# Loads of the inverses' layout issued from GpSimd's queue, with two planner estimates changed, in a hybrid decoder layer

## The chip, the core and the metric

The kernel runs on one core of one Trainium2 chip. That core has five engines which run side by side, each through its own list of instructions and strictly in the order of that list: TensorE (PE in the profile, with PEld for its weight loads), VectorE (DVE), ScalarE (ACT), GpSimd (POOL) and SyncE (SP, which here only starts transfers). Any of SP, ACT and POOL can start a DMA transfer; the instruction that starts it takes its place in that engine's list. The metric is the device time of one execution in microseconds (us).

## The reference

The layer takes x (1024 tokens by 2048), normalises it, multiplies it by one combined projection `W_in`, and feeds the columns to three groups of heads: a spatial gMLP (4 groups of 128 channels), a gated DeltaNet (8 heads of 128) and a cross-attention into 256 memory tokens (4 heads of 128). Each group's output is gated by SiLU of its own columns, all is multiplied by `W_out`, added to x and normalised. The part that the change touches is the DeltaNet. Cut to that:

```python
qkv = causal_conv_silu(concat([d_q, d_k, d_v]), conv_w)      # width-4 convolution over tokens
q, k = l2norm(q) * DN_HEAD_DIM ** -0.5, l2norm(k)
# gated_delta_rule, in chunks of C = 64 tokens
a = where(strict, einsum('bhnid,bhnjd->bhnij', k * beta, k) * decay, 0.0)
T = triangular_solve(a + eye, eye, left_side=True, lower=True, unit_diagonal=True)   # inverse of I + a
value       = einsum('bhnij,bhnjd->bhnid', T, v * beta)
k_cumdecay  = einsum('bhnij,bhnjd->bhnid', T, k * beta * exp(g_cum))
attn_intra  = where(tri, einsum('bhnid,bhnjd->bhnij', q, k) * decay, 0.0)
def step(state, inp):                     # one chunk after the other, along the sequence
    v_new = val_c - k_cumdecay_c @ state
    o_c   = q_g_c @ state + attn_intra_c @ v_new
    state = state * exp(g_last) + k_dec_c.T @ v_new
```

All is in float32, which the kernel makes of products of high and low parts (three matmuls for one, `ahi,whi`, `ahi,wlo`, `alo,whi` in the profile).

## The kernel before, in words

**Who sets the order.** No engine's list is written by hand. The kernel's body calls `S`, `G`, `V`, `PE`, `Q` (ACT, POOL, DVE, PE, SP), and these only record each operation in a `Plan`, with the earlier operations that it depends on. When all is recorded, `Plan.issue` walks through the operations as a planner would: at each step it takes the engine that is free first and, of that engine's operations whose inputs are there by its own clock, the one with the lowest class (`rank(n)` sets the class; 1 is urgent, 9 is the main matmul stream) and then the earliest recorded. It appends this one to the engine's list. What it thinks of times are the estimates in `Plan.price`: `o.cost` is how long an operation occupies its engine, `o.lat` how much later its result is there. For transfers there is also a size term: those of SP and POOL share one modelled channel, those of ACT have a channel of their own at half its rate. On the chip, the lists are then run as they stand: an estimate that is off costs no correctness, but moves operations to other places in the lists, on every engine. All recorded operations are issued through one line, so the profile shows line 280 for nearly everything, and the tiles' names tell them apart.

**Stages.** From 0 to about 165 us the memory tokens are projected and x is normalised. From then to about 500 us the kernel projects the columns of DeltaNet heads 0 to 3, first for tokens 0 to 511 ("half 0", inverses named 00 and 01, two heads each) and then for tokens 512 to 1023 ("half 1", 10 and 11), and runs the DeltaNet on them between the projections' matmuls. From there to about 1310 us five rounds of products (`blocks`) compute the remaining columns by a seven-product scheme; between these matmuls lie the fronts of the late heads 4 to 7 (near 690 and 880 us), one joint inverse for all of these, their recurrences (near 1000 to 1200 us), the gMLP and the attention. From about 1310 us to the end the output projection runs, with no DeltaNet work in it.

**One pair of heads.** `front` does the convolution (`conv`: ACT copies a finished bank of the projection, `xr<-acc`, then three DVE passes), the norms, the decays and, for two heads, the tile `gt` (128 partitions by 8 chunk pairs by 128) that holds the matrices `a`. `blocks_out` then sends the 32x32 blocks on the diagonal of `gt` to DRAM, in four transfers from ACT's queue (`gdr<-gt`), of 32 KB each in pieces of 128 bytes. `inverse` loads them again in another layout, one 32x32 block to a partition, in four transfers (`gd` in the code, a slot of the ring `inv`, so `inv<-gdr` in the profile; 8 partitions by 1024 numbers each), prepares an identity `ti` on POOL, and inverts all blocks at once in 31 steps of two DVE instructions. The results go to DRAM (`tdr`, `udr`, again from ACT's queue). `levels` loads them into place and assembles the 128x128 inverses `ut` by four groups of small matmuls with ACT copies between (`tblk`, `y1`, `y2`). `scan_step`, once for each chunk pair of 128 tokens, is the recurrence: matmul `dn<-states,kT`, then DVE `steps<-dn,sc,vs`, matmul `dn<-steps,ut`, then ACT `steps<-dn`, matmuls `dn<-steps,kd` and `dn<-steps,ai`, and DVE `states<-states,sc,dn`. The joint inverse of the late heads is the same code with four pairs, so 16 loads and 128 partitions.

The loads `gd` run on ACT's queue before, and are recorded with class 1; so are the four stores ahead of them. There are 32 of those stores in the program (8 pairs) and 32 of these loads. The planner's estimates that the change touches stand in `price` at the name "dma_start": the cost of issuing a transfer on each engine, and the latency of a transfer into DRAM.

Of the kernel before, what the change touches and what calls it, by code (L numbers as in the profile page):

```python
# [62 lines left out]
class Plan:  # L63
# [21 lines left out]
    @contextmanager  # L85
    def rank(self, cls):
        old, self.cls = self.cls, cls
        yield
        self.cls = old
# [91 lines left out]
    def price(self, o, name, outs, ins):  # L181

        out = outs[0]
        n = math.prod(out.shape[1:])
        both = [*outs, *ins]
        psum = any(i.space == PSUM for i in both)
        pointer = any(i.shape[-1] == 1 and math.prod(i.shape[1:]) == 1 for i in ins[1:])
        o.nbytes = o.lock = 0
        o.lat = 0.0
        if name == "dma_start":  # L190
            o.cost = {"sp": 380.0, "act": 100.0, "pool": 800.0}[o.eng]
            rows = math.prod(out.shape[:-1])
            o.nbytes = max(4 * math.prod(out.shape), 512 * rows)
            src = ins[0]
            pieces = src.shape[-1] < 128 or out.shape[-1] < 128
            if out.space == DRAM:
                o.lat = 3000.0
            elif pieces or out.shape[0] < 32:
                o.lat = 2400.0
            elif list(src.ap)[0][0] == 0:  # L200
                o.lat = 4000.0
        elif o.eng == "pe":
            passes = 1 if ins[0].dtype == F32R else 2 if name == "transpose" else 4
            o.cost = max(13.3 + n / 2.4 * passes, 222.0 if passes == 4 else 110.0) if out.shape[0] == P else 30.0
            o.lat = 175.0
        elif o.eng == "act":
            o.cost = (165.0 if psum else 200.0) + 0.82 * n + (105.0 if pointer else 0.0)
            o.cost += 190.0 if "accum_out" in o.kw else 0.0
        elif o.eng == "dve":
            n = max([n] + [math.prod(i.shape[1:]) for i in ins])  # L210
            o.cost = (n + 151) / 0.96 + (60.0 if pointer and name == "scalar_tensor_tensor" else 0.0)
            o.lock = not psum and (name.startswith("tensor_") or name == "scalar_tensor_tensor")
            o.lock = o.lock and name != "tensor_reduce"
        else:
            o.lock = 1
            if name in ("memset", "affine_select"):
                o.cost = 100.0 + 0.83 * n * (1 if name == "memset" else 1.4)
                o.lat = 800.0 if name == "affine_select" else 0.0
            else:
                o.cost = 750.0 + 150.0 * (n - 1) if n < 8 else 200.0 + 2.1 * n  # L220
# [63 lines left out]
def kernel(  # L284
# [21 lines left out]
    x, mem, w_in, out = x[0], mem[0], w_in[0], out[0]  # L306
# [7 lines left out]
    V, S, G, PE, Q = R.dve, R.act, R.pool, R.pe, R.sp  # L314
# [5 lines left out]
    def DT(shape, name, dt=F32):  # L320
        return dr.tile(list(shape), dt, name=name, tag=name)[:]
# [35 lines left out]
    def bc(ap, n):  # L357
        return ap.unsqueeze(ap.ndim).to_broadcast(list(ap.shape) + [n])

    def rep(ap, n):  # L360
        return ap.unsqueeze(1).to_broadcast([ap.shape[0], n, ap.shape[1]])
# [618 lines left out]
    def flat(start, *aps):  # L980
        start(*(a.rearrange("p a b -> p (a b)") for a in aps))

    def inverse(gdrs, n, cls):

        nr = 32 * len(gdrs)
        gd = ring["inv"]()[0:nr].rearrange("p (a b) -> p a b", b=32)
        for i, gdr in enumerate(gdrs):
            for b in range(4):
                with rank(1):
                    flat(S.dma_start, gd[i * 32 + b * 8 : i * 32 + (b + 1) * 8], gdr[b])  # L990
        ti = ring["inv"]()[0:nr].rearrange("p (a b) -> p a b", b=32)
        tmp = (y1 if nr == 32 else y2)[0:nr].rearrange("p c m -> p (c m)")
        with rank(4):
            G.memset(ti, 0.0)
            G.affine_select(out=ti, in_=ti, compare_op=ALU.not_equal, fill=1.0, base=0,
                            pattern=[[1, 32], [-1, 32]], channel_multiplier=0)
        with rank(cls):
            for j in range(31):
                n1, m = 31 - j, j + 1
                tv = tmp[:, 0 : n1 * m].rearrange("p (n m) -> p n m", m=m)  # L1000
                V.tensor_tensor(out=tv, in0=bc(gd[:, j, j + 1 :], m), in1=rep(ti[:, j, 0:m], n1), op=ALU.mult)
                V.tensor_tensor(out=ti[:, j + 1 :, 0:m], in0=ti[:, j + 1 :, 0:m], in1=tv, op=ALU.add)
            V.tensor_copy(gd.rearrange("p i m -> p m i"), ti)
        tdr, udr = ([DT([32, 32, 32], f"{t}{n}_{i}") for i in range(len(gdrs))] for t in ("tdr", "udr"))
        for i in range(len(gdrs)):
            with rank(1):
                flat(S.dma_start, tdr[i], ti[i * 32 : (i + 1) * 32])
                flat(S.dma_start, udr[i], gd[i * 32 : (i + 1) * 32])
        return list(zip(tdr, udr))
# [181 lines left out]
    def inverted(n, *states):  # L1191
        return [(*s[:-1], i) for s, i in zip(states, inverse([s[-1] for s in states], n, 3))]
# [324 lines left out]
    with rank(2.6):  # L1517
        late_inv = inverse(gdrs, "late", 1.9)
# [265 lines left out]
```

## Time and profile before

| | |
|---|---|
| median of 3 runs | 1671.42 us (1670.85, 1671.42, 1673.37) |
| span of the profiled execution | 1664.6 us |
| mean granted TensorE clock in it | 0.992 of full speed |
| PE busy | 1623.0 us, 98% of the span |
| DVE busy | 1317.2 us, 79% |
| ACT busy | 1023.2 us, 61% |
| POOL busy | 108.1 us, 6% |
| moved by DMA | 419.50 MB, 252 GB/s |

The profile gives for the profiled execution its span and no other time; the median of the runs is 6.8 us above that span. Times in the timeline count from the span's start. A line of a timeline reads: start, duration, engine (ACTq is an issue of a transfer on ACT), line, operation, output<-inputs, shape, how many alike follow each other, and in brackets the idle time of the engine ahead of it with what ended that. A line of a table by windows reads: window, its length, then busy time and instructions of PE, PEld, DVE, ACT, POOL, then the granted clock of PE, the busy share of the DMA engines and the GB/s. In a table of waits a line gives total us, how many, and the longest.

### The profile page before, as it was taken

Reading aid. Unit: us, or ns where it says so; the run is one execution under the profiler, and the core shown is the slowest. Engines: PE = TensorE matmul, PEld = TensorE weight load, DVE = VectorE, ACT = ScalarE, POOL = GpSimd, SP = SyncE. Lnnn points to the kernel's source line nnn. Section 1 sums busy time; section 2 is a strip of 40 time slices with the busy share of each in tenths; the row PEclk is TensorE's granted clock in tenths of the full one; section 3 lists DMA queues with packets and bytes.
Section 4 is the critical chain, followed back from the end, with each engine's and each line's share of the span. In section 5 each row is a group of like instructions: output and inputs, shape, how many; then the busy total and the mean of one; then the engine's idle time right before and its main releaser. Section 6 shows DMA issues by size and latency. Waiting matters only on the chain.

```text
span 1664.6 us, 26198 instructions
## 1 busy us (share of the span) xinstructions
PE 1623.0 (98%) x8570; PEld 1355.5 (81%) x8570; DVE 1317.2 (79%) x2288; ACT 1023.2 (61%) x2235; POOL 108.1 (6%) x139
## 2 busy tenths in 40 slices
PE   8999999989999999999998999999999999999997
PEld 6888888878878888788886887888888888888886
DVE  4866696939779789889996988786878897688875
ACT  6957674656754457776674447676566774345445
POOL 0000100101010001010010011000000000000001
PEclk9999999999999999999998999999999999999999
DMA  8878887885886877679876877888868869679746
GB/s 273 253 235 267 270 254 225 245 235 180 266 286 208 256 247 250 201 264 326 291 245 206 264 233 242 261 279 282 301 220 291 269 219 359 213 254 304 226 141 240
DMA packets 316658, 419.50 MB, mean 252 GB/s; under 512 B 57773, under 2 KB 138342, under 8 KB 316522
## 3 DMA queue, kind: packets, MB, share of 16 engines
q1 hardware_dynamic: 304834, 410.48, 76.4%
q10 hardware_dynamic: 10600, 5.26, 1.2%
q0 software_dynamic: 1088, 2.10, 0.4%
q8 instruction: 67, 1.10, 0.3%
q14 instruction: 69, 0.57, 0.1%
HBM read 334.33 MB, written 82.87 MB: 251 GB/s over the span
## 4 chain that ended last, share of the span: by engine, by line
PE 72%; DMA 7%; DVE 5%; ACT 2%; issue 2%; ACTq 0%; SPq 0%; POOL 0%; POOLq 0%; DVEq 0%
PE acc L280 54%; PE dn L280 18%; DMA wraw<-in_w_in_dram 1%; DVE alo L280 1%; DMA E<-gcd 1%; DVE y L280 1%; DVE wlo L280 1%; DMA inv<-gdr 1%; DMA y<-in_w_in_dram 1%; ACTq L280 0%; ACT ahi L280 0%; DMA raws<-sd 0%; DVE ai L280 0%; DVE inv L280 0%; DMA zg<-hTd 0%
## 5 line engine op out<-in xcount | busy, mean ns | idle before, releaser
L280 PE MATMUL acc<-ahi,whi 128*128 128x512 f32 (+1 forms) x1152 | 452.9, 394 | 3.3 <-ACT xr L280 1.8
L280 PE MATMUL acc<-alo,whi 128*128 128x512 f32 (+1 forms) x1152 | 452.8, 393 | 0.0
L280 PE MATMUL acc<-ahi,wlo 128*128 128x512 f32 (+1 forms) x1152 | 451.5, 392 | 0.4 <-DVE small L280 0.4
L280 PEld LDWEIGHTS acc<-ahi,whi 128*128 128x128 f32 x1152 | 217.9, 189 | 46.8 <-ACT xr L280 3.1
L280 PEld LDWEIGHTS acc<-ahi,wlo 128*128 128x128 f32 x1152 | 217.7, 189 | 41.2 <-DVE wlo L280 0.6
L280 PEld LDWEIGHTS acc<-alo,whi 128*128 128x128 f32 x1152 | 217.9, 189 | 40.5
L280 PE MATMUL acc<-ahi,zh 128*128 128x512 f32 x736 | 232.1, 393 | 0.0
L280 ACT CAST whi<-wraw 128x512 fp32r<-128x512 f32 (+1 forms) x170 | 137.2, 809 | 112.6 <-PE acc L280 67.7
L280 DVE TENSOR_TENSOR alo<-raws,ahi 128x1024 fp32r<-128x1024 f32 x131 | 160.0, 1222 | 39.3 <-ACT ahi L280 38.9
L280 DVE TENSOR_TENSOR wlo<-wraw,whi 128x1024 fp32r<-128x1024 f32 (+1 forms) x138 | 135.0, 979 | 61.2 <-ACT whi L280 58.4
L280 ACT CAST ahi<-raws 128x1024 fp32r<-128x1024 f32 x131 | 137.4, 1049 | 67.0 <-PE dn L280 28.1
L280 PEld LDWEIGHTS acc<-ahi,zh 128*128 128x128 f32 x736 | 137.0, 188 | 27.1
L280 PE MATMUL acc<-ahi,zl 128*128 128x512 f32 x368 | 144.7, 393 | 0.0
L280 DVE TENSOR_TENSOR ahi<-y,ahi 128x1024 fp32r<-128x1024 f32 x65 | 79.3, 1220 | 23.9 <-ACT ahi L280 23.6
L280 ACT CAST ahi<-y 128x1024 fp32r<-128x1024 f32 x65 | 68.2, 1049 | 37.4 <-PE acc L280 18.3
L280 PEld LDWEIGHTS acc<-ahi,zl 128*128 128x128 f32 x368 | 69.2, 188 | 13.5
L280 ACT CAST zh<-wraw 128x1024 fp32r<-128x1024 f32 x36 | 37.8, 1051 | 44.1 <-PE acc L280 19.9
L280 POOL TENSOR_TENSOR small<-small,mhalf 128x1 f32<-128x1 f32 x26 | 18.6, 721 | 676.9 <-DVE small L280 676.9
L280 POOL TENSOR_TENSOR hs<-hs,mhalf 128x4 f32<-128x4 f32 x32 | 48.4, 1516 | 204.4 <-DVE hs L280 203.4
L280 ACT CAST whi<-y 128x1024 fp32r<-128x1024 f32 x34 | 35.8, 1052 | 38.8 <-issue 20.4
L280 PE MATMUL dn<-wlo,ahi 128*128 128x512 f32 x152 | 59.0, 389 | 0.0
L280 PE MATMUL dn<-whi,alo 128*128 128x512 f32 x152 | 59.0, 389 | 0.0
(397 smaller groups left out, 3221.1 us busy)
## 6 DMA issues: line engine op xcount, KB each, us to landing
wraw<-in_w_in_dram SPq DMA_DIRECT2D x268, 256.0 KB
raws<-sd SPq DMA_DIRECT2D x148, 256.0 KB
y<-in_w_in_dram SPq DMA_DIRECT2D x92, 256.0 KB
y<-sd SPq DMA_DIRECT2D x77, 256.0 KB
wraw<-in_w_out_dram SPq DMA_DIRECT2D x64, 256.0 KB
raws<-h0d SPq DMA_DIRECT2D x54, 256.0 KB
y<-in_w_out_dram SPq DMA_DIRECT2D x33, 256.0 KB
low<-wlo SPq DMA_DIRECT2D x32, 256.0 KB
```

Source lines behind the costliest of these rows:

```text
L280: o.fn(*o.args, **o.kw)
```

## The change

Three edits. `inverse` issues its loads from POOL (`G`) where ACT (`S`) did. In `price`, the estimated cost of issuing a transfer goes from 100 to 430 ns on ACT and from 800 to 1000 ns on POOL. And a transfer into DRAM whose shape is (32, 8, 32), which only the four stores of `blocks_out` have, is estimated to land 9000 ns after its issue and size term, where it was 3000. The arithmetic, the tiles and the sizes of all transfers stay as they are.

```diff
@@ class Plan, def price
         if name == "dma_start":
-            o.cost = {"sp": 380.0, "act": 100.0, "pool": 800.0}[o.eng]
+            o.cost = {"sp": 380.0, "act": 430.0, "pool": 1000.0}[o.eng]
             rows = math.prod(out.shape[:-1])
             o.nbytes = max(4 * math.prod(out.shape), 512 * rows)
             src = ins[0]
             pieces = src.shape[-1] < 128 or out.shape[-1] < 128
             if out.space == DRAM:
-                o.lat = 3000.0
+                o.lat = 9000.0 if out.shape == (32, 8, 32) else 3000.0
@@ def inverse
         for i, gdr in enumerate(gdrs):
             for b in range(4):
                 with rank(1):
-                    flat(S.dma_start, gd[i * 32 + b * 8 : i * 32 + (b + 1) * 8], gdr[b])
+                    flat(G.dma_start, gd[i * 32 + b * 8 : i * 32 + (b + 1) * 8], gdr[b])
```

## The prediction

> **What bounds the kernel now.** I read the page's engine shares and its chain of waits first, then the windows, the table of what TensorE waits for, and the timelines of ACT and PE around each wait.
>
> ```profile
> PE 1623.0 (98%) x8570; PEld 1355.5 (81%) x8570; DVE 1317.2 (79%) x2288; ACT 1023.2 (61%) x2235; POOL 108.1 (6%) x139
> PE 72%; DMA 7%; DVE 5%; ACT 2%; issue 2%; ACTq 0%; SPq 0%; POOL 0%; POOLq 0%; DVEq 0%
> ```
>
> TensorE bounds it: 98% busy, 72% of the chain. Only what makes PE wait, or run at a lower clock, costs time. The windows show how little that is, and where:
>
> ```profile
> 280.00:320.00 40.00, 38.21 (x216) 32.29 (x216) 34.52 (x107) 24.99 (x82) 3.68 (x3) 1.00 0.76 230
> 370.00:375.00 5.00, 5.00 (x23) 4.43 (x23) 2.23 (x11) 1.01 (x5) 0.00 (x0) 0.70 0.71 221
> 490.00:495.00 5.00, 3.82 (x14) 2.82 (x14) 4.76 (x12) 3.58 (x8) 0.69 (x1) 0.75 1.05 386
> 890.00:900.00 10.00, 3.71 (x9) 2.54 (x10) 6.83 (x11) 4.28 (x8) 0.00 (x0) 0.59 0.90 290
> 900.00:905.00 5.00, 5.00 (x20) 3.90 (x19) 3.19 (x6) 3.30 (x5) 0.00 (x0) 0.79 0.66 203
> 1440.00:1480.00 40.00, 40.00 (x179) 33.10 (x178) 27.01 (x33) 14.69 (x17) 0.00 (x0) 1.00 0.64 209
> ```
>
> Where nothing disturbs (1440 to 1480) 179 wide matmuls take 40 us, 0.2235 us each: my unit for distances in the lists. Three places that the change touches run at a clock under 1. In each, PE waited for a copy by ACT (table of PE's waits, then PE's timeline):
>
> ```profile
> PE dn L280 <- ACT gt L280: 7.1, 2, 5.3
> PE dn L280 <- ACT ut L280: 2.6, 1, 2.6
> PE dn L280 <- ACT vs L280: 2.1, 1, 2.1
> ```
>
> ```profile
> 368.21 0.71 PE L280 MATMUL dn<-vs,ut 128*128 128x128 f32 x4 [2.62 <-ACT ut L280]
> 491.18 1.21 PE L280 MATMUL dn<-ident,vs 128*128 128x128 f32 x4 [2.08 <-ACT vs L280]
> 894.51 0.48 PE L280 MATMUL dn<-ident,gt 128*128 128x128 f32 x1 [5.34 <-ACT gt L280]
> 898.04 0.48 PE L280 MATMUL dn<-ident,gt 128*128 128x128 f32 x1 [1.78 <-ACT gt L280]
> ```
>
> ACT's timeline tells why those copies were late: an inverse's load stands just ahead of each, and ACT sits in front of it, idle.
>
> ```profile
> 366.96 0.27 ACTq L280 DMA_DIRECT2D inv<-gdr  x1
> 367.27 0.62 ACT L280 CAST whi<-wraw 128x512 fp32r<-128x512 f32 x1 [2.52 <-DMA wraw<-in_w_in_dram]
> 474.22 3.58 ACTq L280 DMA_DIRECT2D inv<-gdr  x2
> 477.85 0.27 ACT L280 COPY vs<-dn 128x128 f32<-128x128 f32 x1 [3.41 <-DMA inv<-gdr]
> 884.69 3.49 ACTq L280 DMA_DIRECT2D gdr<-gt  x4
> 893.56 0.27 ACTq L280 DMA_DIRECT2D inv<-gdr  x1
> 893.87 0.59 ACT L280 COPY gt<-acc 128x512 f32<-128x512 f32 x1 [1.25 <-DMA wraw<-in_w_in_dram]
> 897.09 0.27 ACTq L280 DMA_DIRECT2D inv<-gdr  x1
> 897.40 0.59 ACT L280 COPY gt<-acc 128x512 f32<-128x512 f32 x1 [2.95 <-DMA raws<-sd]
> ```
>
> The issue itself takes 0.27 us; what costs is the waiting. Twice it ends with a transfer that SP had started for other tiles (`wraw`, `raws`), so it isn't only the store of the same blocks that these loads wait for. [...]
>
> **The change, part by part: what it removes.** The loads leave ACT, so the copies no longer stand behind them. I count the gap that PE showed, and after it busy time times the missing clock.
>
> Late inverse (890 us): 5.34 + 1.78 us of gaps, and 3.71 x 0.41 + 5.00 x 0.21 = 2.6 of clock: 9.7. But the four stores stay on ACT. In the changed program's list the copies `gt`, `steps` and `states` stand ahead of them, and `vs<-dn` and `et<-dn` behind them. TensorE wants the latter about 15 matmuls, 3.4 us, after the first store. The four stores hold ACT for 3.49 us and the two copies take 0.6 each (next fence): 3.49 + 1.2 - 3.4 = 1.3 us of new wait. Left: **-8.4**.
>
> At 368 us: 2.62 + 5.00 x 0.30 = **-4.1**. At 491 us: 2.08 + 3.82 x 0.25 = **-3.0**; ACT was held there at 474 to 481 and had not caught up when the product stage began. Removed together: **-15.5**.
>
> [...]
>
> **What it adds.** All lists shift, since the planner now holds the inverses' steps back until 9 us and more after their stores. Counted in the lists of both programs, in wide matmuls ahead of the event, the first step of the five inverses moves from 580, 873, 1115, 1503 and 3101 to 583, 929, 1181, 1572 and 3212, and the first small matmul of `levels` from 839, 1086, 1361, 1827 and 3462 to 875, 1130, 1461, 1951 and 3576. So the consumers move back with the inverses, with main matmuls in between: no wait is planned from it. Two places are left where less lies in between. For the first, the hops of the recurrence in the timeline of half 0, as they are with 6 to 8 wide matmuls in each:
>
> ```profile
> 295.19 0.60 PE L280 MATMUL dn<-states,kT 128*128 128x128 f32 x4
> 295.71 0.59 DVE L280 SCALAR_TENSOR_TENSOR steps<-dn,sc,vs 128x128 f32<-128x128 f32 x2
> 297.01 0.60 PE L280 MATMUL dn<-steps,ut 128*128 128x128 f32 x4
> 297.43 0.50 ACT L280 ACTIVATE steps<-dn 128x128 f32<-128x128 f32 x2
> 298.82 0.61 PE L280 MATMUL dn<-steps,kd 128*128 128x128 f32 x4
> 904.66 0.60 ACT L280 ACTIVATE et<-dn 128x512 f32<-128x512 f32 x1
> ```
>
> First, at the end of half 0 the recurrence of pair 00 now has four hops in a row with no main matmul between. A bare hop idles PE from the end of its group to the end of the small operation at least: 296.30 - 295.79 = 0.5 us over DVE, 297.93 - 297.61 = 0.3 over ACT; so 1.6 for the four. At most it is the whole distance seen between groups, 1.2 each, 4.8. DVE is 34.52 of 40 us busy there, so other work often stands ahead: I take the middle, **+3**. In the late recurrences the count of hops with little between falls from 11 to 3; I leave that unpriced, 0 to -3.
>
> Second, ACT's copies that empty the projection's banks (`xr<-acc`): in the old list they stand at matmuls 1191, 1221 and 1268, in the new one at 1220, 1220 and 1268. Two full banks now wait together. The nearest place today is a pair four matmuls apart:
>
> ```profile
> 310.19 0.50 PE L280 MATMUL acc<-ahi,whi 128*128 128x512 f32 x1 [0.97 <-ACT xr L280]
> 311.75 0.50 PE L280 MATMUL acc<-ahi,whi 128*128 128x512 f32 x1 [0.82 <-ACT xr L280]
> 307.67 0.73 DVE L280 SCALAR_TENSOR_TENSOR qT<-xr,cw,qT 128x512 f32<-128x512 f32 x1
> 308.33 0.40 DVE L280 TENSOR_TENSOR y<-inv,inv 32x252 f32<-32x252 f32 x1
> L280 DVE TENSOR_TENSOR y<-inv,inv 32x31 f32<-32x31 f32 (+25 forms) x155 | 51.2, 330 | 2.0 <-DMA inv<-gdr 0.2
> ```
>
> At least one such gap more, 0.8. At most both (1.8), three convolution passes of 0.73 that free an `xr`, five inverse steps of 0.40 between them, and 1.5 of clock as at 370 us: 7.5. I take the middle, **+4**.
>
> Third, POOL takes 32 issues. The groups by line have the prices (the three numbers are ns of one: least, median, most):
>
> ```profile
> L280 POOL DMA_DIRECT2D inv<-kvd x2: 722/811/900, 984.5 to 985.4; - x2
> L280 POOL TENSOR_TENSOR hs<-hs,mhalf x32: 1007/1436/3662, 134.3 to 1241.8; 128x4 f32<-128x4 f32 x32
> L280 ACTq DMA_DIRECT2D inv<-gdr x32: 270/281/320, 197.4 to 897.1; - x32
> ```
>
> At 0.81 us, 32 issues are 26 us on an engine that is 6% busy: hidden. If that cover were gone, one issue costs 0.5 more than ACT's 0.28. Behind the loads in POOL's list stand the identity `ti`, two memsets of `ut` and the small powers `hs<-hs,mhalf`, for which DVE and then ACT's `kd` and `vs` wait; a load that waits for a store that has not landed holds them. The planner's 9 us after the store make that unlikely. For the late chain, 50 wide matmuls instead of 54 lie between the last store of an inverse and its first use: 4 x 0.2235 = 0.9. Bounds 0 to 3; I take **+1**. SP's list keeps its transfers; they only move with the rest. The raised issue costs act through the order alone, which the two places above hold.
>
> **Sum:** -15.5 + 3 + 4 + 1 = -7.5 us on the profiled execution of 1664.6. The profile has no time for that execution but the span; the median of 1671.42 stands 6.8 above it, and I carry that over: 1663.9.
>
> **Rivals.** (a) The order's losses stay at their lower ends, 1.6 + 0.8 + 0, and the late recurrences give 3: -15.5 + 2.4 - 3 = -16: 1655. For it: the low ends come from uncrowded hops. Against: DVE is crowded.
>
> (b) The change does only its late part. The two early gaps may come back as waits behind ACT's stores, which hold ACT as long (3.49 us for four) as these loads did. Then -8.4 + 8 is nothing: 1671.
>
> (c) Slower: DVE is late at the end of half 0. The second inverse starts 56 matmuls, 12.5 us, later, and its 62 instructions need 31 x 2 x 0.33 = 20 us of an engine which has 40 - 34.52 = 5.5 us spare in that stretch. If 12.5 - 5.5 = 7 us do not fit, PE waits for them, and bare hops and paired banks go to their upper ends: -15.5 + 7 + 4.8 + 7.5 + 1 = +5: 1676. It decides once that stretch costs over 14.5. For it: DVE's 86%. Against: the consumers moved back too.
>
> (d) POOL's issues stretch. The power `hs` took 1.0 to 3.66 us for the same shape, so something holds POOL at times. Stretched likewise, 3.6 times 0.81 = 2.9 us each, the 16 late loads take 47 us; in the new list they stand between matmuls 3096 and 3197, 22.6 us apart, and the inverse starts 15 matmuls (3.4 us) later. So the inverse is 47 - 26 = 21 us late, and if PE waits for all of it the time is 1664 + 21 = 1685. It decides from 26/16 = 1.6 us for an issue. Against: the two issues of the row above took 0.72 and 0.90.
>
> [...]
>
> **How the numbers follow.** A kernel like this, by its three runs, tells a change of about 0.2%, 3.3 us, from none. Chances: the sum above 0.43, own range 1657 to 1668; (a) 0.14; (b) 0.14; (c) 0.21; (d) 0.08. Faster 0.43 + 0.14 = 0.57, same 0.14, slower 0.29. The range takes in (a) with 5 us of the unpriced, and (c) with 5 more for a second place like it: 1650 to 1681.
>
> **What would show it.** Right: no PE gap behind `gt`, and no clock under 0.9 at the late fronts; ACT without `inv<-gdr`; 32 POOL issues near 0.8 us. The end of half 0 shows 2 to 5 us of PE gaps behind `steps` and `states`, and a gap behind `xr`. Wrong: POOL issues over 1.6 us; `y<-inv,inv` waiting for `inv<-gdr` while PE waits; DVE near 100% with PE gaps before 350 us; or the old gaps behind ACT's stores.

## The result, and the profile after

The changed kernel takes 1665.68 us (median of 20 runs, 1658.74 to 1671.69), the kernel before 1670.78 us in as many (1664.55 to 1676.07). The ratio is 0.9974, with a 95% interval of 0.9962 to 0.9985: faster by 0.26%, 4 to 5 us. 1663.9 was forecast.

The profiled execution of the changed kernel has a span of 1666.5 us; its time is known, 1668.24, and of the next run they are 1663.9 and 1665.59. So 1.7 us lie around a span. For the kernel before this means that the profiled execution (1664.6) took 1666.3 and was 4.5 us faster than its median: the two spans, set side by side, would have the change come out slower. Stages can be compared between the traces, the sum can't.

First the engine shares and the chain of the changed kernel's page, then what its TensorE waited for:

```profile
PE 1629.0 (98%) x8570; PEld 1361.7 (82%) x8570; DVE 1322.0 (79%) x2288; ACT 1024.0 (61%) x2235; POOL 133.3 (8%) x171
PE 75%; DMA 6%; DVE 5%; ACT 2%; issue 1%; SPq 1%; ACTq 0%; POOLq 0%; POOL 0%; DVEq 0%
```

```profile
PE acc L280 <- ACT xr L280: 9.2, 3, 3.9
...
PE dn L280 <- ACT et L280: 2.5, 2, 2.0
...
PE dn L280 <- ACT tn L280: 1.5, 1, 1.5
```

The waits on `gt` (7.1 us), `ut` (2.6) and `vs` (2.1) of before are gone from the top of the list. In their place stand 9.2 us on `xr`, the copies that empty the projection's banks, and waits on `et` and `tn`; the kernel before waited 1.8 us on `xr`, 0.4 on `et`, and not on `tn`. The same by windows (us, busy times, then the granted clock): the late fronts and the two early places, and then the new places.

```profile
370.00:375.00 5.00, 5.00 (x31) 4.35 (x30) 3.89 (x9) 2.47 (x6) 0.00 (x0) 1.00 0.51 106
490.00:495.00 5.00, 5.00 (x28) 4.23 (x27) 3.70 (x9) 1.95 (x4) 2.21 (x2) 1.00 0.72 227
880.00:920.00 40.00, 39.49 (x195) 32.62 (x194) 36.56 (x59) 27.43 (x58) 12.41 (x20) 1.00 0.88 277
```

```profile
65.00:80.00 15.00, 12.04 (x79) 9.77 (x78) 13.65 (x27) 14.16 (x33) 2.30 (x5) 0.98 0.51 117
312.00:330.00 18.00, 12.59 (x53) 9.88 (x53) 16.89 (x45) 10.85 (x36) 3.39 (x3) 0.81 0.55 158
405.00:420.00 15.00, 11.09 (x55) 9.03 (x54) 13.48 (x31) 10.66 (x34) 2.74 (x2) 0.89 0.19 59
1008.00:1028.00 20.00, 16.49 (x90) 13.24 (x89) 13.49 (x24) 10.16 (x19) 2.29 (x4) 0.74 0.69 181
```

The late fronts, where the clock was 0.59 and PE stood more than 7 us, now run at full clock with 0.5 us idle in 40. Four other places have lost what these won. POOL's 32 issues are cheap (groups by line: us in total, mean ns):

```profile
L280 POOL DMA_DIRECT2D inv<-gdr x32 | 17.0, 538 | 7.9 <-PE dn L280 2.7 <-DMA gdr<-gt 2.5 <-ACT ut L280 2.2
```

### The profile page after: what moved, and what is told of

Same layout as the page of the kernel before. It is cut to its first block, busy times and chain, and to the rows that moved or that the text cites. A ratio compares the mean times of both kernels' runs of the same rounds, so it can differ in the third digit from the quotient of the medians.

```text
span 1666.5 us, 26200 instructions
## 1 busy us (share of the span) xinstructions
PE 1629.0 (98%) x8570; PEld 1361.7 (82%) x8570; DVE 1322.0 (79%) x2288; ACT 1024.0 (61%) x2235; POOL 133.3 (8%) x171
## 4 chain that ended last, share of the span: by engine, by line
PE 75%; DMA 6%; DVE 5%; ACT 2%; issue 1%; SPq 1%; ACTq 0%; POOLq 0%; POOL 0%; DVEq 0%
PE acc L280 56%; PE dn L280 18%; DMA wraw<-in_w_in_dram 2%; DVE alo L280 1%; DVE y L280 1%; DMA y<-in_w_in_dram 1%; DVE wlo L280 1%; SPq L280 1%; ACT whi L280 0%; ACT ahi L280 0%; DMA late<-kd 0%; ACTq L280 0%; DMA xr<-pd 0%; DVE zl L280 0%; DVE kT L280 0%
## 5 line engine op out<-in xcount | busy, mean ns | idle before, releaser
L280 PE MATMUL acc<-ahi,whi 128*128 128x512 f32 (+1 forms) x1152 | 454.9, 395 | 13.2 <-ACT xr L280 9.2
L280 PE MATMUL dn<-whi,ahi 128*128 128x512 f32 x152 | 58.8, 389 | 0.0
```

The lines of the kernel that those rows point to most:

```text
L280: o.fn(*o.args, **o.kw)
```

## The experiments

The change has two effects which can be taken apart: which engine issues the loads, and in which order everything stands after the planner has planned with other estimates. The planner can be told one engine and the instruction be put on another, at the same place. So there are two rivals. Theory "queue": the gain is ACT freed of loads that wait, and the new order gives part of it back. Theory "order": the gain is that the planner holds the loads until their stores have landed, and the engine doesn't matter. Ratios below are against the kernel before, run alongside: its median was 1670.87 us beside experiments 1 to 4, 1673.47 beside 5, 6, 7 and 10, and 1672.81 beside 8, 9, 11 and 12. So medians of different groups can lie 2 to 3 us apart for no reason in the kernel, and where much hangs on it the ratio decides. In microseconds ratios are taken of 1671.

**1. The order of before, the loads from POOL.** On the kernel before:

```diff
-                    flat(S.dma_start, gd[i * 32 + b * 8 : i * 32 + (b + 1) * 8], gdr[b])
+                    flat(lambda *t: R.add("act", "dma_start", nc.gpsimd.dma_start, t, {}),
+                         gd[i * 32 + b * 8 : i * 32 + (b + 1) * 8], gdr[b])
```

> The planner plans with the old estimates and believes the 32 loads to be on ACT, but they are issued from POOL at the same places. The lists of PE, DVE and SP are those of the kernel before; only ACT loses the loads and POOL gets them. Theory 'queue' (the gain is ACT freed of waiting loads, the new order costs about half of it): the gaps before 368, 491 and 894 us go, none of the bare hops or paired banks come; 1670.8 - 15.5 + 1 = about 1656, and faster than the changed kernel (1665.7). Theory 'order' (the gain is that the new order holds the loads until their stores have landed): the wait only moves, from ACT to POOL and from there to the inverses' first steps; 1668 to 1672.

Measured: 1651.63 us, ratio 0.9884 (0.9858 to 0.9911), 19 us faster than before and 14 us faster than the changed kernel. Theory "queue" holds, and its gain was set too low. Windows of this kernel at the three places, then POOL's idle time ahead of the loads (us, times, until what), then ACT and POOL at the late fronts:

```profile
365.00:370.00 5.00, 5.00 (x30) 4.34 (x29) 2.81 (x13) 2.04 (x7) 0.00 (x0) 1.00 1.08 380
486.00:491.00 5.00, 5.00 (x28) 4.17 (x27) 4.83 (x12) 4.56 (x12) 0.00 (x0) 1.00 1.06 403
875.00:895.00 20.00, 20.00 (x95) 16.30 (x94) 15.23 (x29) 12.66 (x19) 3.52 (x5) 1.00 0.89 282
```

```profile
  DMA gdr<-gt: 24.3, 6
```

```profile
875.91 3.33 ACTq L280 DMA_DIRECT2D gdr<-gt  x4
...
883.59 1.08 ACT L280 COPY gt<-acc 128x512 f32<-128x512 f32 x2
```

```profile
881.09 2.14 POOL L280 DMA_DIRECT2D inv<-gdr  x4 [4.71 <-DMA gdr<-gt]
```

The wait has not gone: POOL now stands 24.3 us in all in front of loads whose stores have not landed, 4.71 of it at the late fronts. But nothing that PE needs is behind it there, and ACT copies both `gt` tiles without a stop.

This also bears on a reading in the prediction, that ACT's loads wait for more than their own stores. The four stores of the inverse at 368 us are issued at the same time in both kernels (first the kernel before, then experiment 1):

```profile
351.69 3.24 ACTq L280 DMA_DIRECT2D gdr<-gt  x4
...
363.80 0.28 ACTq L280 DMA_DIRECT2D inv<-gdr  x1
364.13 0.63 ACT L280 ACTIVATE vs<-acc,hs 128x128 f32<-128x128 f32 x2 [1.14 <-DMA gt<-gt]
```

```profile
351.56 2.61 ACTq L280 DMA_DIRECT2D gdr<-gt  x4
```

```profile
356.39 2.15 POOL L280 DMA_DIRECT2D inv<-gdr  x4 [1.39 <-DMA gdr<-gt]
```

On POOL the four loads follow in one piece from 356.39 us, when their stores had landed. On ACT they stand alone at 361.54, 363.80, 366.96 and 367.30, and ACT idles 1.14 and 2.52 us at the second and the third, with transfers of other tiles (`gt<-gt`, `wraw`) ending the wait. So at this place it was not the stores that held ACT. The trace puts the wait down to those other transfers; why a load from ACT's queue stands until they end, no run here shows.

**2. The new order, the loads from ACT.** On the changed kernel:

```diff
-                    flat(G.dma_start, gd[i * 32 + b * 8 : i * 32 + (b + 1) * 8], gdr[b])
+                    flat(lambda *t: R.add("pool", "dma_start", nc.scalar.dma_start, t, {}),
+                         gd[i * 32 + b * 8 : i * 32 + (b + 1) * 8], gdr[b])
```

> The opposite: the lists of PE, DVE and SP are those of the changed kernel, and the 32 loads are issued from ACT at the places which the planner gave them on POOL. Theory 'queue': the order alone loses, 1670.8 + 8 = about 1679 if the waits on ACT come back in full, 1673 if half. Theory 'order': the loads stand so far behind their stores that they wait for nothing on ACT either; about 1666, as the changed kernel, with no gap over 1 us behind an ACT copy at the late fronts.

Measured: 1673.08 us, ratio 1.0009 (0.9992 to 1.0025): no difference from before that can be told, and 7 to 8 us slower than the same order with the loads on POOL. In this order the queue is worth less than half of what it is worth in the old one. ACT also stands less around the loads: its idle time there, added up from its timeline, is about 18 us, against 27 in the kernel before. TensorE's waits show the new places again, and 4.2 us on `et` behind ACT's transfers at the late fronts:

```profile
PE acc L280 <- ACT xr L280: 9.6, 3, 3.9
PE dn L280 <- ACT et L280: 6.3, 2, 4.2
```

**3. The changed kernel once more,** for a second profile, with no edit.

> The changed kernel once more, for a second profile: its first profile lost some 7 us more than the kernel before in the first 160 us, where nothing of the inverses runs. If this is the order (the raised issue cost of ACT's transfers also moves the start), it comes again, 5 to 8 us; if it is chance, this profile loses 9 to 12 us there, as the kernel before did. Time 1665 to 1667. The gaps behind xr of 3.7 and 3.9 us (at 318 and 409 us) belong to the order by every theory, and are expected again within 1 us.

Measured: 1665.07 us, ratio 0.9965 (0.9949 to 0.9981). The gaps behind `xr` come again, so they belong to the order, though not all within 1 us: at 322 us it is 2.40 where it was 3.69, at 412 again 3.91. At the start it was both: of the 7 us, part was chance (a dip of the clock at 18 us that this profile doesn't have), part comes again, the gaps at 68 to 77 us with a dip behind them (windows of this profile and of experiment 1, which has the old order):

```profile
65.00:82.00 17.00, 14.03 (x89) 12.03 (x88) 15.96 (x32) 14.35 (x34) 0.92 (x1) 0.90 0.63 160
```

```profile
65.00:80.00 15.00, 13.88 (x107) 12.72 (x107) 14.55 (x28) 14.59 (x36) 1.53 (x1) 1.00 0.73 175
```

**4. The move alone, with the old estimates.** On the kernel before, `S.dma_start` becomes `G.dma_start` in `inverse`, and the planner plans with that.

> One edit alone: the loads go to POOL, all estimates stay (100, 800, 3000). The planner now makes a third order. Theory 'queue': most of the gain of the move is here already, since ACT waits for no load; 1656 to 1666, by where this order puts the bank copies. Theory 'order': without the latency of 9000 the loads are put 6 us too early, POOL and then DVE wait for them, and the time is 1670 or more.

Measured: 1668.45 us, ratio 0.9977 (0.9962 to 0.9992). Between the two expectations, and 17 us slower than experiment 1, though the loads run on the same engine: the planner made another order, and that order cost nearly all of the gain. Its profile shows `xr` gaps of 2.7 and 2.0 us at 314 to 321 us, one of 4.5 behind `vs` at 376 and one of 6.3 behind `et` at 991.

**5. The stores' latency back at 3000.** On the changed kernel:

```diff
-                o.lat = 9000.0 if out.shape == (32, 8, 32) else 3000.0
+                o.lat = 3000.0
```

> The changed kernel with the stores' latency back at 3000: loads from POOL, issue costs 430 and 1000. If the raised issue costs make the new order lose at the start (gaps of 0.6, 0.6 and 1.5 us at 68 to 77 us, then 3.4 us at half clock), these come again here, 4 to 5 us. If the 9000 ns are what set the banks of the projection free in pairs (gaps behind xr of 2, 3 to 4 and 4 us), they go, and the time is 1656 to 1660. If any change of the estimates loses, whichever it is, 1664 to 1670.

Measured: 1657.45 us, ratio 0.9893 (0.9857 to 0.9930), faster than the change as a whole by 8 us in the medians and by 13.5 in the ratios. The gaps at the start come again, as the raised issue costs would have it (`tn`). The `xr` gap at 313 stays at 2.9 us, so the latency isn't what makes that one; the one at 409 is gone, and the one at 256 is down to 0.7.

```profile
PE acc L280 <- ACT xr L280: 3.6, 2, 2.9
...
PE dn L280 <- ACT tn L280: 1.6, 1, 1.6
```

**6. The issue costs back at 100 and 800.** On the changed kernel:

```diff
-            o.cost = {"sp": 380.0, "act": 430.0, "pool": 1000.0}[o.eng]
+            o.cost = {"sp": 380.0, "act": 100.0, "pool": 800.0}[o.eng]
```

> The changed kernel with the issue costs back at 100 and 800: loads from POOL, latency 9000. If the issue costs make the loss at the start, the first 160 us are those of the kernel before (no gap over 0.6 at 73 to 80 us). If the latency makes the paired banks, the gaps behind xr stay, 8 us in all with 3.4 us or more at half clock, and the time is 1661 to 1666. If any change of the estimates loses, 1664 to 1670, with gaps at other places.

Measured: 1677.63 us, ratio 1.0020 (1.0002 to 1.0038): slower than any number I gave. At the start PE is as busy as in the kernel before, 13.88 us of 15 (window below), so its loss does come from the issue costs. Of the gaps behind `xr` the one at 313 us stays, at 3.5; experiment 4, which has neither estimate, has 2.7 there, so neither makes it. The one at 256 is down to 0.9 and the one at 409 is gone, as in experiment 5: these two come only with both estimates. The largest loss lies elsewhere: 8.3 us on `et`, where ACT did nothing for 12.55 us but issue the last seven of the eight stores of the late inverse's results (`tdrlate`, `udrlate`).

```profile
65.00:80.00 15.00, 13.88 (x107) 12.72 (x106) 14.56 (x28) 14.57 (x35) 1.52 (x1) 1.00 0.72 174
```

```profile
1002.87 2.88 ACTq L280 DMA_DIRECT2D tdrlate<-inv  x3
1009.87 5.70 ACTq L280 DMA_DIRECT2D udrlate<-inv  x4
1015.61 1.14 ACT L280 CAST whi<-kT 128x512 fp32r<-128x512 f32 x2 [12.55 <-DMA tblk<-tdrlate]
```

```profile
PE dn L280 <- ACT et L280: 8.3, 1, 8.3
PE acc L280 <- ACT xr L280: 5.2, 3, 3.5
```

**7. The estimates alone, the loads on ACT.** The changed kernel with `S.dma_start` in `inverse`, planned and issued there.

> The estimates alone: loads on ACT, planned and issued there, with 430, 1000 and 9000. The planner now knows that the stores land late, and puts ACT's loads behind other work. If the estimates cure ACT's waits as well as the move does, ACT idles less than 10 us in all ahead of the work behind these loads (27 before), and the time is 1660 to 1666; if the order's loss is all that is left of it, 1670 to 1676, as with the changed order and the loads on ACT (1673.1).

Measured: 1657.71 us, ratio 0.9902 (0.9869 to 0.9934), faster than both expectations. ACT's idle time around the 32 loads, added up from its timeline, is 28 us, as before (27), so by this sum the estimates cure no wait. They move it, and PE's waits say that it is mostly to where PE wants little from ACT. At the late fronts ACT stands longer than ever, 9.44 us in one piece, and PE loses 3.9 us behind it:

```profile
906.52 0.60 ACT L280 ACTIVATE et<-dn 128x512 f32<-128x512 f32 x1 [9.44 <-DMA inv<-gdr]
```

```profile
PE acc L280 <- ACT xr L280: 5.9, 3, 3.6
...
PE dn L280 <- ACT E L280: 3.9, 1, 3.9
```

**8. The order of experiment 7, the loads from POOL.** The planner is told ACT, as in experiment 1, but plans with the new estimates.

> The order of the estimates alone (1657.7 with the loads on ACT), but with the loads issued from POOL at the same places; PE, DVE and SP keep their lists. Theory 'queue' says that ACT's waits are worth what PE loses behind them: here the gap of 3.9 us at 905 with its 3.4 us at half clock and little else, so 1650 to 1653. If the loads already stand where nothing waits for ACT, the queue is worth nothing in this order and the time stays at 1656 to 1659.

Measured: 1656.72 us, ratio 0.9905 (0.9870 to 0.9940), the same as with the loads on ACT. The wait on `E` at the late fronts falls from 3.9 to 1.3 us, as theory "queue" says, yet the time does not follow. In this profile the waits on `vs` and behind a load of `wlo` are 1.0 and 0.6 us longer, the granted clock dips after the one on `vs` (0.83 from 385 to 395 us, where experiment 7 has 1.00 around that wait), and the chance dip at the start is there. Which of these the other runs have too is left open.

**9. The order of before, the loads from SP.** Experiment 1 with `nc.sync.dma_start`.

> The order of the kernel before, the 32 loads issued from SP at the same places. If it is enough that ACT is freed, the time is that of the loads on POOL, 1648 to 1656. If the empty queue matters, SP now stands 24 us in all before these loads (what POOL stood in the old order), and the transfers of weights behind them come late: each wait of 4 us or more that is not covered by loads already in flight shows as a PE or ACT gap behind wraw or raws; 1656 to 1668.

Measured: 1661.01 us, ratio 0.9943 (0.9921 to 0.9966): half of POOL's gain. So ACT freed is worth something without POOL's queue, and the move from SP to POOL is worth as much again. Whether that second half comes of the transfers that stand behind the loads in SP's list, or of something else, these runs don't tell apart. The largest new wait is 2.6 us behind `whi`, which is made from SP's loads:

```profile
PE acc L280 <- ACT whi L280: 3.1, 2, 2.6
```

**10. The order of before, loads and stores from POOL.** Experiment 1, and in `blocks_out`:

```diff
-                S.dma_start(gdr[b].rearrange("c j i -> j c i"), gv[sl, :, sl])
+                R.add("act", "dma_start", nc.gpsimd.dma_start,
+                      (gdr[b].rearrange("c j i -> j c i"), gv[sl, :, sl]), {})
```

> The order of the kernel before, with the loads and also the 32 stores ahead of them issued from POOL, at the same places. ACT then loses the last of its waits around these transfers: the gaps behind jk (1.2 us at 353), inv (2.6 at 681) and et (1.3 at 901) go, with some half clock: 1651.6 - 6 = 1646 if a POOL issue of 1024 pieces of 128 bytes costs about as much as one of a load (0.52). If making the pieces takes POOL longer, 3 us or more for one store, the four of a pair take 12 us and more, the loads and the inverse start later by 9, and PE waits for them at some of the five places: 1652 to 1665.

Measured: 1646.32 us, ratio 0.9830 (0.9797 to 0.9864), the fastest of all. A store in 128-byte pieces (256 of them in 32 KB, not the 1024 that were expected) costs POOL hardly more than a load (least, median, most in ns):

```profile
L280 POOL DMA_DIRECT2D gdr<-gt x32: 584/584/791, 190.4 to 872.8; - x32
L280 POOL DMA_DIRECT2D inv<-gdr x32: 499/511/578, 194.1 to 877.2; - x32
```

**11. All transfers of the inverses from POOL.** Experiment 10, and the two stores of `tdr` and `udr` in the same way.

> The order of the kernel before, with every transfer of the inverses issued from POOL: the loads, the 32 stores ahead of them and the 16 stores of the results. Against 1646.3 without the last 16: ACT idles some 8 us less ahead of them, but TensorE waits only for y at 986 (1.5 us) near one; so 1644 to 1647. If POOL's list gets too full, the small powers between the stores come late, and the time rises over 1648.

Measured: 1648.57 us, ratio 0.9875 (0.9831 to 0.9918). The interval overlaps that of experiment 10, so no gain of the last 16 stores can be told; the median lies just over the 1648 that were given for a POOL list that gets too full. The wait on `y` that was to go is 2.7 us in this profile, where experiment 10 has 1.5. Why it stays isn't shown.

**12. The kernel before once more,** with no edit.

> The kernel before once more, for a second profile: the first was 4.5 us faster than its median. The gaps that the prediction priced (5.3, 1.8, 2.6 and 2.1 us, each behind a load of ACT) come again within 2 us each if they belong to the order; the 4 to 5 us more of a median run are then somewhere else, or these gaps are longer. Span 1664 to 1673.

Measured: 1669.60 us, ratio 0.9987 (0.9968 to 1.0007), span 1665.3. The four gaps come again, within 1.1 us each (those behind `gt` as 6.3 and 0.7, where they were 5.3 and 1.8):

```profile
PE dn L280 <- ACT gt L280: 7.0, 2, 6.3
...
PE dn L280 <- ACT ut L280: 2.9, 1, 2.9
...
PE dn L280 <- ACT vs L280: 2.3, 1, 2.3
```

This profile too was faster than a median run, so what the other runs lose was not seen.

Set side by side, by the medians:

| order of the lists | loads on ACT | loads on POOL |
|---|---|---|
| before | 1670.8 | 1651.6 |
| the change's | 1673.1 | 1665.1 to 1665.7 |
| the estimates' alone | 1657.7 | 1656.7 |

The ratios of the last row, 0.9902 and 0.9905, agree. Neither theory holds by itself. In the three orders the queue is worth 19 us, 8 us, and nothing that can be told. That this goes by how much PE wants from ACT behind the loads is read from PE's waits and not tested by itself. The orders lie as far apart as the queues do: up to 15 us with the loads on ACT, where the estimates' order is the best, and up to 14 with the loads on POOL, where the old one is.

## Why the prediction was right

**What is removed (-15.5).** Right in mechanism and in place: all three gaps went, their dips with them, and the new wait behind ACT's stores at the late fronts was there (0.5 us on `et` where 1.3 were priced). In the two profiled executions the queue alone is worth 1664.6 - 1649.3 = 15.3 us, the forecast. Matched matmul by matmul, these two profiles give 4.2 us at 368 (4.1 priced), 4.5 at 491 (3.0) and 8.6 at the late fronts, a wait of 1.3 on `et` included (8.4); some 2 us go the other way in small pieces. By the medians the queue is worth 19: the terms were taken from an execution that was faster than the median of its kernel. What the slower runs lose besides wasn't found.

**What the order adds (+8).** Right in sign, too small: 1665.1 - 1651.6 = 13.5 us. For each stretch of the same matmul work I took the time that PE needed less what its instructions take undisturbed, in the second profile of the changed kernel and in experiment 1. The differences, which come to the 13.2 us between the two spans:

| place in the changed kernel | lost, us | priced |
|---|---|---|
| 68 to 80, start | 4.2 | nothing |
| 256, first wait on `xr` | 3.0 | nothing |
| 314 to 330, bare hops, then a wait on `xr` | 5.9 | 3, for the hops |
| 408 to 417, paired banks | 4.7 | 4 |
| 1008 to 1028, `y` and `et` | 7.5 | nothing |
| after it, to 1100 | 1.7 | 1 |
| everywhere else | -13.8 | 0 to -3 |

Both priced places came where the lists had put them. The paired banks stand at 410 and 413 us: both copies have 1216 wide matmuls ahead of them in the first profile of the changed kernel (1220 by the lists), and in the kernel before 1186 and 1217. They cost 4.7 us for the 4 taken. ACT's copies there, then PE's wait for them:

```profile
409.97 0.58 ACT L280 COPY xr<-acc 128x512 f32<-128x512 f32 x1
...
412.63 0.56 ACT L280 COPY xr<-acc 128x512 f32<-128x512 f32 x1
```

```profile
413.25 0.50 PE L280 MATMUL acc<-ahi,whi 128*128 128x512 f32 x1 [3.91 <-ACT xr L280]
```

The hops at the end of half 0 were near their low end of 1.6 us, with gaps of 0.35, 0.28 and 0.77. What makes that stretch dear is the wait after them, on the copy of a bank: 3.69 us with 6.8 us at half clock in the first profile (18 us at 0.81), 2.40 in the second. This copy stands behind 928 wide matmuls in both kernels, and PE waited 0.97 us for it before; the prediction had shown it as its example and didn't price it. PE's timeline in the first profile:

```profile
314.26 0.49 PE L280 MATMUL dn<-states,kT 128*128 128x128 f32 x2 [0.35 <-DVE states L280]
315.02 0.49 PE L280 MATMUL dn<-states,kT 128*128 128x128 f32 x2 [0.28 <-ACT vs L280]
316.28 0.75 PE L280 MATMUL dn<-steps,ut 128*128 128x128 f32 x4 [0.77 <-DVE steps L280]
322.47 0.79 PE L280 MATMUL acc<-ahi,whi 128*128 128x512 f32 x1 [3.69 <-ACT xr L280]
```

The step that failed is "Two places are left where less lies in between". Four more lost time: the start, the first wait on `xr` at 256 us, the wait on `xr` at 322, and 1008 us. For the start the prediction had nothing: "The raised issue costs act through the order alone, which the two places above hold". Experiments 5 and 6 show that its loss is theirs, more than 100 us ahead of the first inverse. The wait at 256 us needs both estimates, the one at 322 neither. The largest, at 1008 us, is a wait behind ACT's other transfers. The eight stores of the late inverse's results stay on ACT, and in the new order they hold it twice for over 3.7 us where before it was 2.5 and 1.1. ACT in the first profile of the changed kernel, then PE in the second:

```profile
1000.33 4.13 ACTq L280 DMA_DIRECT2D tdrlate<-inv  x4
1004.81 5.26 ACTq L280 DMA_DIRECT2D udrlate<-inv  x4
1010.17 1.14 ACT L280 CAST whi<-qT 128x512 fp32r<-128x512 f32 x2 [4.54 <-PE acc L280]
```

```profile
1010.94 0.50 PE L280 MATMUL acc<-ahi,whi 128*128 128x512 f32 x1 [1.81 <-ACT y L280]
1013.95 2.08 PE L280 MATMUL dn<-wsT,el 128*128 128x128 f32 x8 [2.04 <-ACT et L280]
```

That these stores make the gaps of 1.8 and 2.0 us is read from the order of the lines; a changed order with only these stores taken off ACT wasn't tried. The last row of the table, everywhere else, is the part that I had left "unpriced, 0 to -3": the new order was better in the recurrences and in the middle of the products by more than I allowed.

**The sum.** -7.5 was forecast and about -5 measured, within the likeliest case's own range. That it came so near is in good part luck. Both halves were too small, 15.5 for 19 and 8 for 13.5, so that the difference came out better than its terms. And within the second half some 18 us lost at places that were put at nothing stood against 13.8 us won elsewhere, put at 3 at most. 6.8 us were carried from the span to the median: 1.7 of it lies around every span, the rest was this one execution.

**The rivals.** (a) did not come: the order's losses were not at their lower ends. (b) is wrong in its mechanism, the early gaps did not come back behind the stores of the blocks; but a wait behind another group of ACT's stores did. (c) is right that time is lost at the end of half 0, where DVE is 16.89 of 18 us busy, and wrong about the size: 5.9 us, where 14.5 would have decided. (d) is refuted: POOL's issues took 0.52 to 0.74 us beside a DVE as busy as ever (1322.0 us, 1317.2 before). Some 65% of the time of these issues in the first profile lay beside an instruction of DVE, nearly all TENSOR_TENSOR and SCALAR_TENSOR_TENSOR.

## What to carry to other kernels

Here a waiting issue cost what the critical engine wanted from the instructions behind it, as read from PE's waits, and not the time that it waited: in the old order ACT's 27 us of waiting cost 19 us, in the estimates' order 28 us cost nothing that can be told. Where a planner orders everything, an edit of an estimate is an edit of every list; hold the order fixed to see what the intended edit is worth (here 19 us; with a new plan each time, the same move came out anywhere from 3 us slower, experiment 6, to 16 us faster, experiment 5), and look for the new plan's losses far from the edit. Try a waiting issue on an engine with little in its list, and the stores ahead of it too: that version, in the old order, took 1646.3 us.

## What the runs showed of the hardware that was not expected

A GpSimd issue of 32 KB cost nearly the same in the two shapes seen here: 0.52 us for a load in rows of 4 KB and 0.58 for a store in pieces of 128 bytes. The two issues of 512 KB that the prediction priced them by took 0.72 and 0.90.

TensorE's clock fell after some single gaps of about 2 us, for longer than the gap: a mean of 0.79 over the 8 us of the second window below is 3.4 us at half clock (the low value is 0.50, as from 1016 to 1024 us in the first profile of the changed kernel). After the wait on `xr` at 256 us it fell in the second profile of the changed kernel, where the gap was 1.95 us, and not in the first, where it was 1.61. In the first profile of the kernel before it fell after gaps of 1.83 us at 356 us (0.59 over the next 4.2 us) and 2.08 at 491 (0.66 over the next 5), and stayed at 1.00 over the next 9 us after gaps of 1.98 at 691 us and 2.72 at 1009. So near 2 us the length of the gap alone doesn't decide. Windows of the first and of the second profile of the changed kernel:

```profile
255.00:263.00 8.00, 6.39 (x29) 4.96 (x28) 6.02 (x15) 3.75 (x7) 0.00 (x0) 1.00 0.85 258
```

```profile
255.00:263.00 8.00, 6.05 (x20) 4.50 (x19) 6.13 (x15) 3.24 (x6) 0.00 (x0) 0.79 0.84 250
```
